# A larger load allowance in the instruction planner, and grouped output products in the gated linear attention

## The chip, the core and the metric

The kernel runs on one core of one Trainium2 chip. The time is device microseconds of one launch. A core has five instruction queues that the texts speak of: TensorE (PE; its weight loads are shown apart as PEld), VectorE (DVE), ScalarE (ACT), GpSimd (POOL) and SyncE (SP), which only issues DMA transfers. Each queue takes its instructions strictly in the order in which they were issued, and waits for semaphores of the others.

## The reference

One hybrid block in f32 on 512 latent tokens and 256 context tokens of width 1024, with two layers. Layer 0 has a bidirectional chunked gated linear attention (4 heads, 64 key and 128 value columns, chunks of 64 tokens) beside a gated spatial mixing; layer 1 has a bidirectional state-space scan. Every layer has modulated norms, gated residuals and a SwiGLU feed-forward. The part that the second edit touches is the output of the linear attention, for each direction:

```
b = cumsum(log_a, axis=2)
q_dec = q * exp(b)
o_inter = einsum('bnlhk,bnhkv->bnlhv', q_dec, s_prev)
scores = einsum('bnlhk,bnshk->bnhls', q_dec, k * exp(-b))
scores = where(tri, scores, 0.0)
o_intra = einsum('bnhls,bnshv->bnlhv', scores, v)
o = o_inter + o_intra
...
a = group_rms_norm(o, gla_norm_g, GLA_HEADS) * silu(r)
```

## The kernel before

The program is written once as a sequence of operations, and a planner orders them. `Plan._add` records each operation with its engine, its modelled cost and its dependencies; a block under `pl.together()` is recorded as one operation of TensorE, which nothing can be put into. `Plan.schedule` makes three rounds: `_forward` goes through modelled time and gives each engine, whenever it is free, the ready operation with the best key; `_backward` derives new keys from the order found. The order with the shortest modelled span is issued. On the chip nothing of the modelled times is left, only the order on each engine and the semaphores between engines. Since everything is issued from one line, all work shows as line 562 in the profile, and groups are told apart by tile names and shapes.

`LATENCY` is what the planner adds between the end of an operation and the readiness of a consumer on another engine. For "sync", a load, it stands behind the modelled transfer (`_cost`: bytes / 360e3 us, so 1.46 us for 512 KB and 0.73 for 256 KB).

Weights come through four 512 KB slots (`stg`): a load, then a split into two f16 halves, one by ScalarE and the rest by VectorE, into `gran` slots, from which TensorE multiplies in three passes. PSUM has eight banks, which the planner hands out. The adaLN rows are summed by VectorE from loads of `mod_w`.

The linear attention works on six tiles of 128 tokens with two chunks of 64 each. For each tile, scores of both directions are formed by small 64x64 products, and VectorE's masked copies bring them into `k2[i]` and empty the bank. Eleven steps then carry the state along the chunks, in both directions, by short VectorE operations of 64x128 on `S2`. In the output loop a tile's head gets one full product (scores times values, 128 columns of the array) and two half ones (decayed queries of one chunk times that chunk's state, 64 columns each), all into one bank:

```
for h in range(4):
    te.matmul(o[:, h, :], k2[i][:, h, :], vt[i][:, h * P:(h + 1) * P], start=True, stop=False)
    for c in range(2):
        te.matmul(o[64 * c:64 * c + 64, h, :], q2[i][:, h, 64 * c:64 * c + 64], S2[2 * i + c][:, h, :],
                  start=False, stop=True)
```

At the end of the kernel, each finished tile of 128 tokens has its squares summed by ScalarE, a reciprocal root made in short 128x1 steps by VectorE (`rstd_of`), and is multiplied by it and by `fgr`, the final norm's weights. The last tile is done in three pieces, whose products with `fgr` are separate operations.

Of the kernel before, what the change touches and what calls it, by code (L numbers as in the profile page):

```python
# [19 lines left out]
P = 128  # L20
# [200 lines left out]
PATIENCE = 0.14  # L221
MARGIN = 1.0
AHEAD = 4
LATENCY = {"tensor": 0.2, "vector": 0.25, "scalar": 0.35, "gpsimd": 0.3, "sync": 2.2}


class Plan:


    def __init__(self, nc):  # L230
        self.nc, self.ops, self.open, self.after, self.sooner, self.rush = nc, [], None, (), 0.0, 0.0
        for e in LATENCY:
            setattr(self, e, Engine(self, e))
# [22 lines left out]
    def _add(self, eng, calls):  # L256
# [19 lines left out]
        if eng == "sync":  # L276
            op.deps.update(self.after)
        op.lat = LATENCY[eng]
        self.ops.append(op)
# [102 lines left out]
    def _backward(self, order, span):  # L382
# [3 lines left out]
        for t, _, op in order:  # L386
            rank[op.idx] = -t - op.cost
        clock = dict.fromkeys(LATENCY, 0.0)
        ready = [0.0] * len(ops)
        wait = {e: [] for e in LATENCY}  # L390
        can = {e: [] for e in LATENCY}
        for op in ops:
            if not op.succ:
                heapq.heappush(wait[op.eng], (0.0, op.idx))
        for _ in ops:
            t, e = min((clock[e] if can[e] else max(clock[e], wait[e][0][0]), e) for e in LATENCY if can[e] or wait[e])
            while wait[e] and wait[e][0][0] <= t + 1e-9:
# [176 lines left out]
def tile_hybrid_block(ctx: ExitStack, tc: tile.TileContext, t_in: dict, out: bass.AP):  # L574
    nc = tc.nc
    pl = Plan(nc)
    va, sc, gp, te, sy = pl.vector, pl.scalar, pl.gpsimd, pl.tensor, pl.sync
# [37 lines left out]
    def at(off, shape, dt=F32):  # L615
        return area.view(off, shape, dt)
# [63 lines left out]
    o = ring_s((P, P))  # L680
# [4 lines left out]
    o = ring_s((P, 96))  # L685
# [97 lines left out]
    def rstd_of(ss, n, scale):  # L783
        t = smalls((P, 4, n))
        v, y, q, p = (t[:, i] for i in range(4))
        va.tensor_scalar(v, ss, 0.59565131 * scale, 0.59565131 * EPS, ALU.mult, ALU.add)
        va.tensor_scalar(y.bitcast(I32), v.bitcast(I32), -0.5, -553162335.0, ALU.mult, ALU.add)
        for last in (False, True):
            if n == 1:
                va.scalar_tensor_tensor(out=q, in0=y, scalar=y, in1=v, op0=ALU.mult, op1=ALU.mult)  # L790
            else:
                va.tensor_tensor(out=q, in0=y, in1=y, op=ALU.mult)
                va.tensor_tensor(out=q, in0=q, in1=v, op=ALU.mult)
            if last:
                va.scalar_tensor_tensor(out=y, in0=q, scalar=-1.59012754, in1=y, op0=ALU.add, op1=ALU.mult)
            else:
                va.scalar_tensor_tensor(out=p, in0=q, scalar=-1.98524553, in1=q, op0=ALU.add, op1=ALU.mult)
                va.scalar_tensor_tensor(out=y, in0=p, scalar=1.77101678, in1=y, op0=ALU.add, op1=ALU.mult)
        return y
# [116 lines left out]
    def split(src, dst):  # L916
        sc.activation(out=dst[0], in_=src, func=AF.Copy)
        va.tensor_tensor(out=dst[1], in0=src, in1=dst[0], op=ALU.subtract)

    def columns_of(src, dst):  # L920

        return src.rearrange("p (r c) -> p c r", r=8), [t.rearrange("p (c r) -> p c r", r=8) for t in dst]
# [56 lines left out]
    vt = [at(24 * KB + 2 * KB * i, (P, 512)) for i in range(NT)]  # L979
    q2 = [at(36 * KB + 2 * KB * i, (P, 4, P)) for i in range(NT)]  # L980
    k2 = [at(48 * KB + 2 * KB * i, (P, 4, P)) for i in range(NT)]
# [20 lines left out]
    for i in range(NT):  # L1002
        for k0 in (0, 4):
            o = ring_s((P, 4, P))
# [100 lines left out]
    o = ring_m((96, 256))  # L1105
    for kt in range(KT):
        with pl.together():
            for i, (a, b) in enumerate(PASSES):
                for g in range(3):
                    te.matmul(o[32 * g:32 * g + 32], wl[:, a, kt, :], hT(b, kt, slice(256 * g, 256 * g + 256)),  # L1110
                              start=(kt == 0 and i == 0), stop=(kt == KT - 1 and i == 2))
# [7 lines left out]
    for sl in (XS, CS):  # L1119
        n = sl.stop - sl.start  # L1120
        tl = slice(sl.start // P, sl.stop // P)
        for ws, which, scl in ((wk, 1, UN), (wq, 0, UN / 8.0)):
            for j in range(2):
                o = ring_m((P, n))
# [7 lines left out]
    for i in (4, 5, 0, 1, 2, 3):  # L1132
        o = ring_m((P, 512))
# [11 lines left out]
    for it, i in enumerate((4, 5, 0, 1, 2, 3)):  # L1145
# [32 lines left out]
        for c in range(2):  # L1178
            ch = 2 * i + c
            ds = ring_s((P, 4, P))  # L1180
            with pl.together():
                for h in range(4):
                    te.matmul(ds[:, h, :], kpt[64 * c:64 * c + 64, h, :], vt[i][64 * c:64 * c + 64, h * P:(h + 1) * P],
                              start=True, stop=True)
# [4 lines left out]
        for d in range(2):  # L1189
            o = ring_s((P, 4, 64))  # L1190
            with pl.together():
                for h in range(4):
                    for c in (0, 64):
                        te.matmul(o[c:c + 64, h, :], k2[i][64 * d:64 * d + 64, h, c:c + 64], q2[i][64 * d:64 * d + 64, h, c:c + 64],
                                  start=True, stop=True)
# [19 lines left out]
    o = ring_s((P, 4, P))  # L1215
# [7 lines left out]
    for i in range(NT):  # L1223
        o = ring_m((P, 512))
# [8 lines left out]
        o = ring_s((P, 4, P))  # L1233
# [6 lines left out]
    for j in range(4):  # L1240
        wu = w_cols(w_in, 1568 + j * P, P)
        for sl in (XS, CS):
            n = sl.stop - sl.start
            o = ring_m((P, n))
# [10 lines left out]
    for i in range(NT):  # L1255
        o = ring_m((P, 512))
# [5 lines left out]
    for i in range(NT):  # L1262
        o = ring_s((P, 4, P))
        with pl.together():
            for h in range(4):
                te.matmul(o[:, h, :], k2[i][:, h, :], vt[i][:, h * P:(h + 1) * P], start=True, stop=False)
                for c in range(2):
                    te.matmul(o[64 * c:64 * c + 64, h, :], q2[i][:, h, 64 * c:64 * c + 64], S2[2 * i + c][:, h, :],
                              start=False, stop=True)
        ss = smalls((P, 4))  # L1270
        junk, a = ts((P, 4, P)), ts((P, 4, P))
        for h in range(4):
            sc.activation(out=junk[:, h, :], in_=o[:, h, :], func=AF.Square, accum_out=ss[:, h:h + 1])
        r = rstd_of(ss, 4, 1.0 / P)
        for h in range(4):
            va.scalar_tensor_tensor(out=a[:, h, :], in0=o[:, h, :], scalar=r[:, h:h + 1], in1=rg[i][:, h * P:(h + 1) * P],
                                    op0=ALU.mult, op1=ALU.mult)
        if i < 4:
            latents.append(a)
        else:  # L1280
            o = ring_s((P, 4, P))
            with pl.together():
                for h in range(4):
                    te.transpose(o[:, h, :], a[:, h, :], ident)
            split(o, [t[:, :, TOK[i]] for t in aT_a])
        if i == 3:
            for h in range(4):
                o = ring_s((P, SEQ))
                with pl.together():
                    for t, a in enumerate(latents):  # L1290
                        te.transpose(o[:, TOK[t]], a[:, h, :], ident)
                split(*columns_of(o, [t[:, h, XS] for t in aT_a]))
# [30 lines left out]
    for i in range(NT):  # L1323
        for h in range(2):
            o = ring_m((P, 512))
# [121 lines left out]
    o = ring_s((P, 120))  # L1447
# [11 lines left out]
    for i in range(NT):  # L1459
        o = ring_m((P, 64))  # L1460
# [18 lines left out]
    def cum(mats):  # L1479
        o = ring_s((P, 2, NT, 32))  # L1480
        with pl.together():
            for d in range(2):
                te.matmul(o[:, d], mats[d], da[:, :, 32 * d:32 * d + 32], start=True, stop=True)
        return o
# [11 lines left out]
    o = cum(stri[::-1])  # L1496
# [3 lines left out]
    o = cum([ones, ones])  # L1500
    sc.activation(out=dec, in_=o, func=AF.Exp)
    o = ring_s((P, 4, P))
# [231 lines left out]
    for i in ffn(1, hS1, parts1, 4, (7, 7, 8), [(56 + 2 * k) * KB for k in range(8)], [4 * KB * k for k in (0, 1, 3, 4, 5, 8, 10, 11)], {0: gate5},  # L1734
                 pieces, ring_of([*range(40, 48, 2), *range(114, 120, 2)]), 1):
        o = t4[0]((P, D))
# [47 lines left out]
```

## Time and profile before

| | |
|---|---|
| time, median of 3 runs | 1624.97 us (1624.22 to 1628.23) |
| the profiled execution | 1628.33 us, of which the span is 1626.6 |
| TensorE busy | 1569.3 us (96%), granted clock 0.994 of full |
| VectorE busy | 1380.4 us (85%) |
| ScalarE busy | 945.9 us (58%) |
| moved by DMA | 210.53 MB, mean 129 GB/s |

The profiled execution is one run of the program; its span reaches from the first to the last instruction, and a little lies around it. A busy time counts an engine's instructions, not how well it is used by them.

### The profile page before, as it was taken

The numbers are of one execution on the slowest core, as the hardware profiler recorded it, in microseconds if no ns is written. First come the engines' busy times: TensorE is split into PE (matmuls) and PEld (weight loads), VectorE is DVE, ScalarE is ACT, GpSimd is POOL, SyncE is SP. The second block draws the span as 40 slices with busy tenths as digits, with TensorE's granted clock in tenths as the row PEclk, the third lists the DMA queues.
The fourth block names the chain that finished last, engine by engine and source line by source line (L and its number), as shares of the span: only waits on it lengthen the run. The fifth ranks groups of instructions, "written<-read, shape, count | busy, mean of one in ns | idle before, by whom it ended". The sixth has DMA issues, their size and how long they took to land. (4 is left out here: it accounts for less than half of the span.)

```text
span 1626.6 us, 28133 instructions
## 1 busy us (share of the span) xinstructions
PE 1569.3 (96%) x10893; PEld 949.0 (58%) x10893; DVE 1380.4 (85%) x2661; ACT 945.9 (58%) x1902; POOL 20.4 (1%) x65
## 2 busy tenths in 40 slices
PE   5999999999999999999999999999999999999997
PEld 3555655576545545555578555555544687786674
DVE  3899997699999989856569999999998898898775
ACT  6856534476424514523367899998875665464451
POOL 2000000000000000000010000000000000000000
PEclk9999999999999999999999999999999999999999
DMA  9663335015546565312312445454566233443321
GB/s 331 221 200 104 106 105 166 14 43 166 167 133 191 159 207 181 104 52 72 104 55 80 138 128 167 104 143 124 168 210 160 81 103 117 130 121 113 98 59 52
DMA packets 206121, 210.53 MB, mean 129 GB/s; under 512 B 27199, under 2 KB 154275, under 8 KB 205987
## 3 DMA queue, kind: packets, MB, share of 16 engines
q1 hardware_dynamic: 205987, 208.74, 43.0%
q8 instruction: 85, 1.39, 0.4%
q14 instruction: 49, 0.40, 0.1%
HBM read 197.01 MB, written 7.50 MB: 126 GB/s over the span
## 5 line engine op out<-in xcount | busy, mean ns | idle before, releaser
L562 PE MATMUL bank<-area,gran 128*128 128x256 f16 (+3 forms) x5604 | 788.8, 296 | 10.9 <-DVE area L562 6.3
L562 PEld LDWEIGHTS <-gran 128*128 128x128 f16 x5604 | 519.4, 98 | 260.6 <-issue 29.7
L562 PE MATMUL bank<-area 128*128 128x512 f16 (+9 forms) x3170 | 540.3, 327 | 9.6 <-ACT area L562 5.8
L562 PEld LDWEIGHTS <-area 128*128 128x128 f16 (+1 forms) x3270 | 303.3, 98 | 326.8 <-issue 30.2
L562 ACT ACTIVATE gran<-stg 128x512 f16<-128x512 f32 (+2 forms) x366 | 252.4, 699 | 227.7 <-PE bank L562 86.8
L562 ACT ACTIVATE area<-area 128x128 f32<-128x128 f32 (+8 forms) x557 | 249.0, 490 | 134.5 <-DVE area L562 121.0
L562 DVE TENSOR_TENSOR area<-area 128x512 f32<-128x512 f32 (+8 forms) x489 | 295.9, 627 | 28.1 <-ACT area L562 23.0
L562 ACT ACTIVATE area<-bank 128x384 f32<-128x384 f32 (+7 forms) x460 | 204.3, 463 | 180.7 <-PE bank L562 133.4
L562 DVE SCALAR_TENSOR_TENSOR gran<-stg,gran 128x512 f16<-128x512 f32 (+2 forms) x366 | 277.3, 774 | 32.5 <-ACT gran L562 30.4
L562 PE MATMUL bank<-gran,area 128*128 128x512 f16 (+1 forms) x1308 | 283.4, 360 | 4.4 <-DVE area L562 3.5
L562 DVE TENSOR_TENSOR area<-bank,area 128x512 f32<-128x512 f32 (+5 forms) x237 | 135.6, 581 | 70.8 <-PE bank L562 66.1
L562 DVE SCALAR_TENSOR_TENSOR area<-area,cs 128x512 f32<-128x512 f32 x224 | 158.0, 744 | 9.1 <-DMA area<-in_mod_w_dram 8.8
L562 DVE SCALAR_TENSOR_TENSOR area<-area,mrow 128x772 f32<-128x772 f32 (+1 forms) x96 | 91.6, 969 | 0.0
L562 PEld LDWEIGHTS bank<-area 128*64 128x64 f32 (+4 forms) x1208 | 72.9, 149 | 30.9 <-issue 10.3
L562 ACT ACTIVATE area<-stg 128x1024 f16<-128x1024 f32 (+1 forms) x56 | 55.4, 999 | 33.1 <-PE bank L562 15.6
L562 DVE SCALAR_TENSOR_TENSOR area<-stg,area 128x1024 f16<-128x1024 f32 (+1 forms) x56 | 64.2, 1152 | 11.0 <-ACT area L562 10.6
L562 ACT ACTIVATE area<-area,small 128x64 f32<-128x64 f32 (+1 forms) x161 | 62.0, 458 | 17.0 <-DVE small L562 16.1
L562 PE MATMUL bank<-ident,area 128*128 128x128 f32 (+1 forms) x351 | 51.5, 286 | 12.1 <-DMA area<-in_ssd_norm_g_dram 6.1
L562 DVE TENSOR_TENSOR stg<-stg,stg 128x512 f32<-128x512 f32 x88 | 60.2, 684 | 1.9 <-DMA stg<-in_ffn_w_in_dram 1.2
L562 DVE TENSOR_TENSOR stg<-stg 128x512 f32<-128x512 f32 x88 | 60.2, 684 | 0.5
L562 PEld LDWEIGHTS bank<-ident,area 128*128 128x128 f32 (+1 forms) x351 | 42.5, 147 | 23.7 <-issue 9.2
L562 DVE SCALAR_TENSOR_TENSOR area<-area 64x128 f32<-64x128 f32 (+3 forms) x148 | 52.5, 396 | 3.1 <-ACT area L562 2.5
(74 smaller groups left out, 567.3 us busy)
## 6 DMA issues: line engine op xcount, KB each, us to landing
area<-in_mod_w_dram SPq DMA_DIRECT2D x96, 512.0 KB, 4.3
stg<-in_ffn_w_in_dram SPq DMA_DIRECT2D x88, 512.0 KB, 4.7
stg<-in_ffn_w_out_dram SPq DMA_DIRECT2D x44, 512.0 KB, 3.7
stg<-in_ssd_w_in_dram SPq DMA_DIRECT2D x40, 512.0 KB, 3.9
area<-rowd SPq DMA_DIRECT2D x32, 512.0 KB, 3.9
stg<-in_ab_w_in_dram SPq DMA_DIRECT2D x20, 512.0 KB, 4.4
stg<-in_ssd_w_out_dram SPq DMA_DIRECT2D x32, 256.0 KB, 2.6
area<-in_x_dram SPq DMA_DIRECT2D x8, 512.0 KB, 5.1
```

Of the source, the lines that this page charges most:

```text
L562: getattr(eng, method)(*map(real, a), **{n: real(v) for n, v in k.items()})
```

## The change

The allowance that the planner adds behind a load goes from 2.2 to 4.0 us. In the output loop of the linear attention, a tile's four full products are issued first and the eight half ones after them; the first product of the bank starts its sum, and the others add to it.

```diff
-LATENCY = {"tensor": 0.2, "vector": 0.25, "scalar": 0.35, "gpsimd": 0.3, "sync": 2.2}
+LATENCY = {"tensor": 0.2, "vector": 0.25, "scalar": 0.35, "gpsimd": 0.3, "sync": 4.0}
...
         with pl.together():
             for h in range(4):
-                te.matmul(o[:, h, :], k2[i][:, h, :], vt[i][:, h * P:(h + 1) * P], start=True, stop=False)
+                te.matmul(o[:, h, :], k2[i][:, h, :], vt[i][:, h * P:(h + 1) * P], start=h == 0, stop=False,
+                          skip_group_check=True)
+            for h in range(4):
                 for c in range(2):
                     te.matmul(o[64 * c:64 * c + 64, h, :], q2[i][:, h, 64 * c:64 * c + 64], S2[2 * i + c][:, h, :],
-                              start=False, stop=True)
+                              start=False, stop=True, skip_group_check=True)
```

The planner's cost and dependencies of the tile's block are the same with both sequences, so its order is that of the first edit alone, but for the rows inside these blocks. The first edit moves instructions on all engines. Three places are shown.

The first place is TensorE's order at the first output tiles of the linear attention (`bank_N` is a PSUM bank, and `area` the scratch memory in which scores, queries, values and states lie). Before, one tile and the start of the next:

```order
L562 MATMUL bank_67<-area 128x128 [waits DVE_49,Pool_49]
L562 MATMUL bank_67<-area 64x128 x2
L562 MATMUL bank_67<-area 128x128
L562 MATMUL bank_67<-area 64x128 x2
L562 MATMUL bank_67<-area 128x128
L562 MATMUL bank_67<-area 64x128 x2
L562 MATMUL bank_67<-area 128x128
L562 MATMUL bank_67<-area 64x128 x2
L562 MATMUL bank_70<-area 128x128 [waits DVE_49,Pool_49]
```

After, two tiles and what follows:

```order
L562 MATMUL bank_69<-area 128x128 [waits DVE_49,Pool_49]
L562 MATMUL bank_69<-area 128x128 x3
L562 MATMUL bank_69<-area 64x128 x8
L562 MATMUL bank_65<-area 128x128 [waits Activation_49,Pool_49]
L562 MATMUL bank_65<-area 128x128 x3
L562 MATMUL bank_65<-area 64x128 x8
L562 LDWEIGHTS area
```

A tile goes through eight changes between full and half products before, and two after.

The second place is VectorE's order at the last scores of the linear attention: masked copies that empty score banks, and steps of the chunk scan (64x128) and additions of both directions (64x4x64) between them. Before:

```order
L562 COPY_PREDICATED area<-area,bank_70 64x4x64
L562 TENSOR_TENSOR area<-area 64x4x64 [waits DVE_49]
L562 SCALAR_TENSOR_TENSOR area<-area 64x128 [waits Activation_49]
L562 SCALAR_TENSOR_TENSOR area<-area 64x128 x3
L562 TENSOR_TENSOR area<-area 64x4x64 [waits DVE_49] x2
L562 SCALAR_TENSOR_TENSOR area<-area 64x128 [waits DVE_49] x12
L562 TENSOR_TENSOR area<-area 64x4x64
L562 SCALAR_TENSOR_TENSOR area<-area 64x128 [waits Activation_49]
L562 SCALAR_TENSOR_TENSOR area<-area 64x128 x3
L562 COPY_PREDICATED area<-area,bank_64 64x4x64 [waits Pool_49]
L562 COPY_PREDICATED area<-area,bank_66 64x4x64 [waits PE_49]
```

After:

```order
L562 COPY_PREDICATED area<-area,bank_68 64x4x64
L562 TENSOR_TENSOR area<-area 64x4x64 [waits DVE_49] x2
L562 SCALAR_TENSOR_TENSOR area<-area 64x128 [waits Activation_49]
L562 SCALAR_TENSOR_TENSOR area<-area 64x128 x3
L562 TENSOR_TENSOR area<-area 64x4x64 [waits DVE_49] x2
L562 SCALAR_TENSOR_TENSOR area<-area 64x128 [waits Activation_49]
L562 SCALAR_TENSOR_TENSOR area<-area 64x128 x3
L562 SCALAR_TENSOR_TENSOR area<-area 64x128 [waits DVE_49] x4
L562 COPY_PREDICATED area<-area,bank_68 64x4x64 [waits PE_49]
L562 COPY_PREDICATED area<-area,bank_68 64x4x64
```

Before, 20 scan steps and four additions stand ahead of the next bank that is emptied; after, 12 and four, and then `bank_68` is emptied alone. TensorE's next score group into `bank_68` stands behind three earlier groups and six products with 256 columns.

The third place is VectorE's order at the end of the kernel: the residual additions of the last tile (reading a bank), the scaling of the tile before it (128x1024), the products with the final norm's weights (last tile, from `area` alone) and the sum over the last tile's pieces (TENSOR_REDUCE). Before:

```order
L562 TENSOR_REDUCE small_87<-small_87 128x1 [waits Activation_49]
L562 SCALAR_TENSOR_TENSOR small_86<-small_86 128x1 [waits DVE_49]
L562 TENSOR_SCALAR small_88<-small_87 128x1 [waits DVE_49]
L562 SCALAR_TENSOR_TENSOR small_86<-small_86 128x1 [waits DVE_49]
L562 TENSOR_SCALAR small_88<-small_88 128x1 [waits DVE_49]
L562 SCALAR_TENSOR_TENSOR area<-area,small_86 128x1024 [waits DMAHW4_49,DVE_49]
L562 SCALAR_TENSOR_TENSOR small_88<-small_88 128x1 [waits DVE_49]
L562 TENSOR_TENSOR area<-area 128x256 [waits DMAHW5_49]
L562 SCALAR_TENSOR_TENSOR small_88<-small_88 128x1 [waits DVE_49]
L562 TENSOR_TENSOR area<-area 128x512
L562 SCALAR_TENSOR_TENSOR small_88<-small_88 128x1 [waits DVE_49]
L562 TENSOR_TENSOR area<-area 128x256
```

After:

```order
L562 SCALAR_TENSOR_TENSOR area<-area,small_86 128x1024 [waits DMAHW4_49,DVE_49]
L562 TENSOR_TENSOR area<-bank_69,area 128x512 [waits PE_49]
L562 TENSOR_TENSOR area<-area 128x512 [waits DVE_49]
L562 TENSOR_TENSOR area<-bank_63,area 128x256 [waits PE_49]
L562 TENSOR_TENSOR area<-bank_70,area 128x256 [waits PE_49]
L562 TENSOR_TENSOR area<-area 128x256 [waits DVE_49] x2
L562 TENSOR_TENSOR area<-area 128x256 [waits DMAHW5_49,DVE_49]
L562 TENSOR_TENSOR area<-area 128x256 [waits DVE_49]
L562 TENSOR_TENSOR area<-area 128x512
L562 TENSOR_REDUCE small_87<-small_87 128x1 [waits Activation_49]
L562 TENSOR_SCALAR small_88<-small_87 128x1 [waits DVE_49]
```

The scaling of the tile before the last stood behind the sum, and now stands ahead of the last residual additions; the three products with the norm's weights stood behind the sum, and now stand ahead of it.

## Rows read from the trace of the kernel before

**Rows 1.** The page's first part: busy us, share of the span, instructions.

```profile
PE 1569.3 (96%) x10893; PEld 949.0 (58%) x10893; DVE 1380.4 (85%) x2661; ACT 945.9 (58%) x1902; POOL 20.4 (1%) x65
```

**Rows 2.** Windows: length, busy us of PE, PEld, DVE, ACT, POOL; clock, DMA share, GB/s.

```profile
0.00:40.00 40.00, 22.06 (x298) 15.49 (x298) 14.67 (x48) 24.65 (x43) 9.47 (x39) 0.91 0.97 332
200.00:240.00 40.00, 36.55 (x327) 21.90 (x326) 38.64 (x96) 13.82 (x33) 2.10 (x4) 0.96 0.26 80
240.00:280.00 40.00, 40.00 (x229) 21.37 (x229) 31.19 (x101) 19.15 (x54) 0.00 (x0) 1.00 0.63 182
280.00:320.00 40.00, 40.00 (x197) 19.24 (x196) 22.90 (x50) 14.78 (x23) 0.00 (x0) 1.00 0.04 16
320.00:1600.00 1280.00, 1259.74 (x8672) 775.20 (x8671) 1101.51 (x1966) 763.92 (x1570) 6.53 (x18) 1.00 0.42 124
880.00:1240.00 360.00, 350.12 (x2224) 191.92 (x2222) 341.75 (x589) 315.50 (x717) 0.00 (x0) 1.00 0.51 147
```

**Rows 3.** Timeline of PE at output tiles: start, us, instruction, count, idle before.

```profile
231.24 9.42 PE L562 MATMUL bank<-area 128*128 128x128 f32 x72
240.59 5.35 PE L562 MATMUL bank<-gran,area 128*128 128x512 f16 x24
245.78 3.12 PE L562 MATMUL bank<-area 128*128 128x128 f32 x24
248.83 8.59 PE L562 MATMUL bank<-gran,area 128*128 128x512 f16 x39
```

**Rows 4.** Timeline of PE at spatial mixing (full) and cumulative sums (half).

```profile
159.34 1.05 PE L562 MATMUL bank<-area 128*128 128x128 f32 x8
160.23 1.03 PE L562 MATMUL bank<-gran,area 128*128 128x512 f16 x4
...
76.13 1.09 PE L562 MATMUL bank<-area 128*64 128x128 f32 x16
77.15 0.82 PE L562 MATMUL bank<-area,gran 128*128 128x512 f16 x3
```

**Rows 5.** Timeline of PE at the last scores.

```profile
207.77 1.62 PE L562 MATMUL bank<-area 64*64 64x64 f32 x48
...
218.18 4.13 PE L562 MATMUL bank<-gran,area 128*128 128x512 f16 x12 [3.19 <-DVE area L562]
222.15 0.82 PE L562 MATMUL bank<-area,gran 128*128 128x256 f16 x6
```

**Rows 6.** Timeline of DVE at the last scores.

```profile
201.94 1.77 DVE L562 TENSOR_TENSOR area<-area 64x256 f32<-64x256 f32 x4
...
205.87 3.73 DVE L562 COPY_PREDICATED area<-area,bank 64x256 f32<-64x256 uint8 x8
...
212.06 3.31 DVE L562 SCALAR_TENSOR_TENSOR area<-area 64x128 f32<-64x128 f32 x12
```

**Rows 7.** Waits: who waited for what, us in total, times, longest.

```profile
ACT gran L562 <- DMA stg<-in_ffn_w_in_dram: 79.2, 47, 6.5
...
PE bank L562 <- DVE area L562: 15.7, 20, 3.2
```

**Rows 8.** Timeline of DVE at the kernel's end.

```profile
1617.82 0.15 DVE L562 TENSOR_REDUCE small<-small 128x1 f32<-128x3 f32 x1
...
1618.38 1.28 DVE L562 SCALAR_TENSOR_TENSOR area<-area,small 128x1024 f32<-128x1024 f32 x1
...
1619.72 0.42 DVE L562 TENSOR_TENSOR area<-area 128x256 f32<-128x256 f32 x1
...
1620.12 0.68 DVE L562 TENSOR_TENSOR area<-area 128x512 f32<-128x512 f32 x1
...
1621.57 0.48 DVE L562 TENSOR_SCALAR area<-area,small 128x512 f32<-128x512 f32 x1
```

**Rows 9.** DMA issues of the page: count, KB each, median us to landing.

```profile
stg<-in_ffn_w_in_dram SPq DMA_DIRECT2D x88, 512.0 KB, 4.7
...
stg<-in_ssd_w_out_dram SPq DMA_DIRECT2D x32, 256.0 KB, 2.6
```

## The prediction

> **What bounds the kernel now.** I begin with the totals per engine on the page [rows 1]: TensorE is busy 1569.3 of 1626.6 us and VectorE 1380.4. So TensorE is the engine whose work sets the length, and a stretch in which it is not busy, or busy with avoidable work, is where time can be had. The windows [rows 2] say where that is: 17.9 us of the first 40 are without TensorE work (loads are awaited there), 3.45 us of 200 to 240, and 20.3 us of the long middle from 320 to 1600, 9.9 of these from 880 to 1240. From 240 to 320 TensorE has no gap, while VectorE has 8.8 and 17.1 us to spare. That matters, since the second edit stands there. The table of waits [rows 7] gives what TensorE waited for: 15.7 us for VectorE in 20 waits. ScalarE waits far longer for loads, 79.2 us in 47 times, but little of that reaches TensorE. The two edits therefore have to be looked at in two ways: the products cut TensorE's own work in a stretch where it sets the pace; the planner's number moves everything else, and its worth lies in the waits.
>
> **The products of the linear attention's output.** In the timeline [rows 3] one token tile is a run of 24 records: an f32 matmul leaves two, so four full products are 8 and eight half ones are 16. Three tiles follow each other from 231.24 to 240.59, 3.12 us each; a fourth takes 245.78 to 248.83, 3.05 us. I take 3.08 for each of the six. What would the same work cost in blocks of one form? Rows of other stages show both forms [rows 4]. Eight records with full columns stand at 159.34 and the next product starts at 160.23: 0.89 us. Sixteen with 64 columns stand at 76.13 and the next starts at 77.15: 1.02 us, which are two to an interval of some 0.11, because the halves write to different columns of the array and run side by side. Together 1.91 us. The 1.17 us that a tile now takes above this go with its eight changes of form (each head goes from full to half and back), 0.146 us each. After the change there are two, into the halves and out of them. If the cumsum row already holds both, a tile costs 1.91; if neither, 2.20. I take 2.0, nearer the row, which stands between f16 products with full columns and so has both changes in it. The gain is 6 x (3.08 - 2.00) = **6.5 us**, with ends 6 x 0.88 = 5.3 and 6 x 1.17 = 7.0. In the order of the change the first two such tiles still stand in a row, and each is one block of 4 and one of 8 rows. Does it reach the end? TensorE has no gap from 240 to 320, so its shorter work moves up what follows, as long as VectorE follows; its 25.9 spare us there [rows 2] hold 6.5, and also the 12 accumulations of the modulation rows that the new order moves to behind this stage.
>
> **The planner's number.** It changes no instruction's work. What it does is to count a 512 KB load's consumer as ready 1.8 us later, so that other work is put ahead of it in the engines' fixed orders, on all engines. Nothing in the kernel then waits for 4 us: an engine takes its next instruction when its semaphores allow it. So only places can be costed where the order shows a different wait.
>
> *Score stage.* Now TensorE waits 3.19 us at 218.18 [rows 5], for a bank that VectorE's masked copies empty, and these stand behind a dozen short scan steps of the linear attention (3.31 us) and some more [rows 6]. The twelve products behind the wait take 3.97 us to the next row, where at the pitch of the same form (24 from 240.59 to 245.78, 0.216 us each [rows 3]) they would take 2.59: for part of them the granted clock is the lower level, 1.2 GHz, after the idle time. That price of 1.4 us any such stall may pay, and I leave it in both kernels. In the order of the change the last score group of a tile (`bank_68`) waits for copies that stand behind four additions of 64x256 (1.77 us) and twelve scan steps (3.31); with two copies at 3.73 / 8 = 0.47 that makes 6.0 us. TensorE, which waits for the copies ahead of these steps, has meanwhile two score groups (three in 1.62 us at 207.77 [rows 5]) and six products of 256 columns (half of 0.216 each), together 1.7 us. The stall would be about 4.3 us instead of 3.2: **+1**, with ends of 0 (if VectorE arrives there earlier in its order than TensorE) and +2.5 (if the lower clock comes on top for longer).
>
> *Tail.* After the last products VectorE now does work of finished tiles inside the chain that ends the kernel [rows 8]. From the sum at 1617.82 to the last scaling at 1621.57 lie short dependent steps, between them a scaling of a whole tile (1.28 us) and three multiplications (0.42 twice and 0.68), 2.8 us of work that isn't the chain's. In the order of the change the tile's scaling stands ahead of the last residual additions, where VectorE waits for TensorE anyway, and the three multiplications stand ahead of the sum. The first goes, about 1.2 us; the others overlap the ScalarE squares that the sum waits for, but hold the sum up by some 0.6. I take **-1.5**, ends 0 and -2.
>
> *Start.* The fourth tile of x is loaded ahead of the modulation weights, and the second eight of these start five places later behind 768 KB of other loads, 2.3 us at the 332 GB/s of the first window [rows 2]; against that, the bias and the first half's scale come earlier, and later loads have less ahead of them. I take **0**, ends -1.5 and +2.4.
>
> *Elsewhere.* The feed-forward and the state-space stages are reordered throughout, with the same work. TensorE's gaps from 320 to 1600 are 20.3 us [rows 2]. I can't say from the order which of them open or close; I take **0** with ends -10 and +10, half of them closed or half as many again. Against the direction of the edit one row speaks: a feed-forward load lands a median 4.7 us after its issue and a 256 KB one of the state-space output 2.6 [rows 9]; the plan counted 3.66 and 2.93 for these, and now 5.46 and 4.73. The truth lies between for the one and below both for the other: by the rows the new number overshoots the feed-forward's landing by 0.8 where the old one undershot it by 1.0. The Trainium skill's page "DMA: Bandwidth & Descriptors", section "Anatomy of one DMA — SWDGE (gpsimd) path", fits a load's time as 2.0 us plus bytes over 436 GB/s; 512 KB would be an estimated 3.2 us, so that the old number fits and the new one counts over 2 us too many for every load. The trace disagrees for the feed-forward's loads (4.7) and agrees for the smaller ones (an estimated 2.6 by the page, 2.6 measured).
>
> **Sum.** -6.5 + 1 - 1.5 + 0 + 0 = -7.0 us, against the profiled execution's 1628.33 (span 1626.6): 1621.3. That execution lies 3.4 above the median of the runs shown, 1624.97, so the forecast for the median is **1618.0**. The likeliest case alone has 1613 to 1623.
>
> **Rivals.**
> - *The plan now holds loaded work back* (slower). Place: 880 to 1240, where TensorE (350.1 of 360), VectorE (341.8) and ScalarE (315.5) are all nearly full [rows 2]. With 256 KB loads there in 2.6 us and counted as 4.73, splits of weights are put behind the scan's work although their load is long in, and TensorE's products wait for the split. If its 9.9 us without work double and some more, +14, the kernel takes 1632. For it: a load of the order of 2 us too early costs nothing, a split too late costs its wait on the full engine. Against it: TensorE's 15.7 us of waits for VectorE [rows 7] have no load as their last cause. It decides from +11.8 on, where 1629.8 is passed.
> - *The replanning also closes gaps.* Feed-forward loads at 4.7 are late by the old count, ScalarE waits 79.2 us for them, and products queue behind the splits. With 8 to 10 of the middle's 20.3 us closed: 1608 to 1610.
> - *The product's gain does not get through.* VectorE has only 1.4 us to spare from 200 to 240 and 18 of the 360 from 880 on [rows 2]. If it, not TensorE, sets the pace there, the 6.5 us shrink to about 1 and the result is 1623.5, within 0.3%. Against it: TensorE is at 40.00 in two windows in between, with VectorE at 31.19 and 22.90.
> - *The regrouping does nothing.* If a half product takes its 0.2 us whatever stands ahead of it, 1624.5. Against it: the cumsum's halves [rows 4] run at half of that.
>
> **How the numbers follow.** A difference under 0.3% (4.9 us: 1620.1 to 1629.8) is no change here. Chances: the forecast 0.44, of which a fifth ends over 1620.1; gaps closed as well 0.18; gain swallowed 0.18; regrouping idle 0.05; held back 0.15, all but a little of it past 1629.8. Faster: 0.35 + 0.18 + 0.02 of the swallowed = 0.55; within: 0.09 + 0.16 + 0.05 + 0.02 of the held back = 0.32; slower 0.13. The range of 8 in 10 reaches from the closed gaps' upper part, 1609, to 1629, which leaves the held-back case and the best of the closed gaps out.
>
> **What would show it.** Products: each of the six runs of 24 records takes 2.0 us (1.91 to 2.20). Scores: TensorE's longest wait near 215 for VectorE goes from 3.2 to about 4.3. Tail: no scaling of a tile between the last sum and the last scaling, and 1.5 us less from the last product to the end. Elsewhere: TensorE's idle time from 320 to 1600 stays within a few us of 20, and ScalarE's waits for feed-forward loads fall without TensorE's waits moving. The prediction is wrong if TensorE's gaps from 880 to 1240 grow or shrink by more than 8 us, or if VectorE has no slack left behind the products.

## The result

The changed kernel takes 1601.9 us (median of 4 runs, 1599.86 to 1602.25) against 1626.6 of before: ratio 0.9844, interval 0.9823 to 0.9866. It is 24.7 us faster. The forecast of 1618.0 had the direction, not the size, and its range ended 7 us above the result. The profiled execution has a span of 1600.5 us, 26.1 less than before's. The first line of its page, with the columns of [rows 1]:

```profile
PE 1557.1 (97%) x10893; PEld 949.7 (59%) x10893; DVE 1380.8 (86%) x2661; ACT 939.6 (59%) x1900; POOL 20.7 (1%) x65
```

VectorE has the work that it had [rows 1]. TensorE is busy for 12.2 us less, and the span shrank by more than that. The windows of the changed kernel, with the columns of [rows 2], show where it also stands still less:

```profile
0.00:80.00 80.00, 61.29 (x605) 38.17 (x606) 52.00 (x112) 56.50 (x99) 10.62 (x41) 0.96 0.86 280
200.00:240.00 40.00, 35.35 (x247) 20.24 (x248) 37.33 (x94) 15.57 (x27) 1.05 (x2) 0.91 0.27 89
320.00:1580.00 1260.00, 1251.23 (x8648) 772.49 (x8647) 1104.01 (x1979) 758.93 (x1570) 6.96 (x18) 1.00 0.43 125
880.00:1220.00 340.00, 337.68 (x2166) 183.64 (x2164) 331.13 (x585) 308.14 (x708) 0.00 (x0) 1.00 0.55 156
```

From 320 us to just before the tail, TensorE is idle for 8.8 us where it was 20.3 [rows 2], and in the state-space part of it for 2.3 instead of 9.9. The fall from 320 us on is the largest piece, and the forecast had put 0 there. The products' tiles, the rows of which answer to [rows 3]:

```profile
230.27 2.08 PE L562 MATMUL bank<-area 128*128 128x128 f32 x24
232.28 1.04 PE L562 MATMUL bank<-gran,area 128*128 128x512 f16 x4
...
251.72 2.08 PE L562 MATMUL bank<-area 128*128 128x128 f32 x24
253.73 3.41 PE L562 MATMUL bank<-gran,area 128*128 128x512 f16 x15
```

A tile takes 2.01 us, read from its first row to the next row, as before's 3.08 were; the two tiles that stand in a row take 4.12 together. The tail, in VectorE's rows that answer to [rows 8]:

```profile
1591.20 0.76 DVE L562 TENSOR_TENSOR area<-bank,area 128x256 f32<-128x256 f32 x2 [0.87 <-PE bank L562]
1591.87 2.02 DVE L562 TENSOR_TENSOR area<-area 128x256 f32<-128x256 f32 x5
1593.81 0.15 DVE L562 TENSOR_REDUCE small<-small 128x1 f32<-128x3 f32 x1
...
1595.46 0.48 DVE L562 TENSOR_SCALAR area<-area,small 128x512 f32<-128x512 f32 x1
```

From the sum to the last scaling pass 1.65 us instead of 3.75, and no tile is scaled in between.

### The profile page after: what moved, and what is told of

It is laid out like the page before. It is cut to its first block, busy times and chain, and to the rows that moved or that the text cites. A ratio compares the mean times of both kernels' runs of the same rounds, so it can differ in the third digit from the quotient of the medians.

```text
span 1600.5 us, 28106 instructions
## 1 busy us (share of the span) xinstructions
PE 1557.1 (97%) x10893; PEld 949.7 (59%) x10893; DVE 1380.8 (86%) x2661; ACT 939.6 (59%) x1900; POOL 20.7 (1%) x65
## 4 chain that ended last, share of the span: by engine, by line
PE 78%; DVE 12%; ACT 6%; DMA 2%; issue 1%; SPq 0%; DVEq 0%; ACTq 0%
PE bank L562 78%; DVE area L562 9%; ACT area L562 5%; DVE gran L562 2%; ACT gran L562 1%; ACT L560 1%; DMA area<-in_mod_b_dram 1%; DMA area<-in_mod_w_dram 1%; ACT L562 1%; DVE small L562 0%; DVE stg L562 0%; DMA area<-area 0%; DMA stg<-in_ffn_w_in_dram 0%; DMA area<-in_x_dram 0%; DMA stg<-in_ssd_w_out_dram 0%
## 5 line engine op out<-in xcount | busy, mean ns | idle before, releaser
L562 PE MATMUL bank<-area,gran 128*128 128x256 f16 (+3 forms) x5604 | 780.7, 296 | 3.0 <-DVE area L562 2.6
L562 PE MATMUL bank<-area 128*128 128x512 f16 (+9 forms) x3170 | 525.8, 326 | 8.4 <-DVE area L562 5.5
L562 PEld LDWEIGHTS <-area 128*128 128x128 f16 x3270 | 303.5, 98 | 324.1 <-issue 19.1
L562 ACT ACTIVATE area<-bank 128x384 f32<-128x384 f32 (+8 forms) x460 | 204.8, 465 | 189.4 <-PE bank L562 140.6
L562 DVE SCALAR_TENSOR_TENSOR area<-area 64x128 f32<-64x128 f32 (+3 forms) x148 | 53.8, 395 | 3.7 <-ACT area L562 2.6
```

The source lines that it names most:

```text
L562: getattr(eng, method)(*map(real, a), **{n: real(v) for n, v in k.items()})
```

## Where the old order lost time: two chains

Before the experiments I looked for a gap of TensorE that the changed kernel no longer has. At 426.61 us of the kernel before, one row of each of three engines shows how a load reaches TensorE without being named as the cause of its wait (the timelines of ScalarE, VectorE and TensorE; in brackets the idle time and who ended it):

```profile
424.74 0.63 ACT L562 ACTIVATE gran<-stg 128x512 f16<-128x512 f32 x1 [2.62 <-DMA stg<-in_ffn_w_in_dram]
...
425.40 0.69 DVE L562 SCALAR_TENSOR_TENSOR gran<-stg,gran 128x512 f16<-128x512 f32 x1 [1.86 <-ACT gran L562]
426.01 0.55 DVE L562 TENSOR_TENSOR area<-bank,area 128x384 f32<-128x384 f32 x1
...
426.61 1.62 PE L562 MATMUL bank<-area,gran 128*128 128x384 f16 x9 [1.50 <-DVE area L562]
```

The plan put the split of a weight tile where its load should have landed. It had not. ScalarE waited 2.62 us at the split, VectorE 1.86 for ScalarE's half, and behind VectorE's half stood an addition that reads a bank. TensorE waited 1.50 us, by the profile for VectorE. A second chain of this kind starts at a load of modulation weights, for which VectorE waits:

```profile
604.46 1.54 DVE L562 SCALAR_TENSOR_TENSOR area<-area,cs 128x512 f32<-128x512 f32 x2 [2.61 <-DMA area<-in_mod_w_dram]
...
609.90 0.75 DVE L562 SCALAR_TENSOR_TENSOR area<-area,cs 128x512 f32<-128x512 f32 x1 [0.66 <-DMA area<-in_mod_w_dram]
...
611.84 0.43 PE L562 MATMUL bank<-area,one 128*32 128x128 f32 x8 [0.87 <-DVE area L562]
```

From these came the theory: with 2.2 the loads were counted as landed too early, the orders put splits and accumulations ahead of work that was ready, and TensorE paid at second or third hand. Its rival: the planner reorders nearly every row at any change of a number, the old order was a poor draw, and any other number would have done as well.

## The experiments

All times are medians; "before" was run beside each on the same chip and took 1625.4 to 1627.4, so kernels that were not run beside each other compare to some 2 us. But for allowance_alone, all kernels have the regrouped products.

**The two edits apart.** The first kernel has the new sequence of products alone; against the changed kernel its edit is

```diff
-LATENCY = {"tensor": 0.2, "vector": 0.25, "scalar": 0.35, "gpsimd": 0.3, "sync": 4.0}
+LATENCY = {"tensor": 0.2, "vector": 0.25, "scalar": 0.35, "gpsimd": 0.3, "sync": 2.2}
```

> Regrouped output products with the allowance left at 2.2. By the prediction's term the six tiles go from 3.08 to 2.0 us and the kernel is 5.3 to 7.0 us faster than before, about 1620 beside 1626.6. Rival, that the products' gain does not get through: within 1 us of before. If it gives more than 10 us, the replanning is not what made the change larger than forecast.

Measured: 1617.2 us, ratio 0.9948 (0.9932 to 0.9963), 8.5 us faster by the ratio, with 6.0 to 11.1 in the interval. Its tiles take what they take in the changed kernel, so the forecast's 6.5 lies in the interval; from 840 to 1240 us TensorE still idles for 9.9:

```profile
241.13 2.08 PE L562 MATMUL bank<-area 128*128 128x128 f32 x24
243.14 8.59 PE L562 MATMUL bank<-gran,area 128*128 128x512 f16 x39
...
840.00:1240.00 400.00, 390.14 (x2665) 224.26 (x2662) 378.53 (x652) 343.79 (x764) 0.00 (x0) 1.00 0.50 143
```

The second kernel has the new allowance alone; against the kernel before its edit is

```diff
-LATENCY = {"tensor": 0.2, "vector": 0.25, "scalar": 0.35, "gpsimd": 0.3, "sync": 2.2}
+LATENCY = {"tensor": 0.2, "vector": 0.25, "scalar": 0.35, "gpsimd": 0.3, "sync": 4.0}
```

> The allowance of 4.0 with the old sequence of products. If replanning closed gaps of TensorE between 320 and 1240 us, as the changed kernel's windows suggest (20.3 us of the middle without work against 8.8), this is 17 to 20 us faster than before, about 1608. If the two edits only help together, under 10 us.

Measured: 1607.55 us, ratio 0.9885 (0.9869 to 0.9901): 18.7 us. So the allowance carries about two thirds or more, and the two edits add up to the whole within their intervals.

**The size of the allowance.** One number of the changed kernel differs (2.0, 2.3, 3.0, 3.9, 5.0 in place of 4.0).

> Both edits, allowance 2.0, further below the measured landing. Theory of the loads' count: 1616 to 1622, slower than or equal to the 1617 of 2.2, with TensorE's gaps from 320 to 840 at 4 us or more. Theory of draws: as likely below 1612 as above.

> Both edits, allowance 2.3, a tenth above the old number. Theory of loads placed too early: the loads are counted almost as early as with 2.2, so the time stays within 4 us of the 1617 that the products alone gave, with ScalarE's waits for feed-forward loads at 60 us or more. Rival, that any new number draws a new order and 2.2 was a poor draw: 5 us or more away from 1617, most likely below it.

> Both edits, allowance 3.0 instead of 4.0: the plan counts 4.46 us for a 512 KB load, near the median of 4.0 to 4.7 measured. Theory of loads placed too early by the old count: nearly all of the gain, 1600 to 1608. Rival, that any new number only shuffles the order: anywhere between 1600 and 1630, with no relation to ScalarE's waits for loads.

> Both edits, allowance 3.9, a tenth below the new number. Theory of loads placed too early: within 4 us of the 1601.9 of the changed kernel. Rival, that 4.0 was a good draw: 5 us or more slower, about 1607 to 1615.

> Both edits, allowance 5.0: the plan counts 6.46 us for a 512 KB load, more than the median landing. Theory of loads placed too early: as fast as with 4.0 within 5 us, since an early load costs nothing while slots are free, and ScalarE's waits for feed-forward loads stay under 30 us. Rival, that too large a number holds loaded work back: slower than with 4.0 by 8 us or more, with TensorE's gaps from 880 to 1220 above 6 us.

Measured, with the time in which TensorE had no work in three stretches (the window's length less its busy time) and ScalarE's wait for feed-forward input weights:

| allowance | time, us | 320 to 840 | 840 to 1240 | 1320 to 1590 | ScalarE's wait |
|---|---|---|---|---|---|
| 2.0 | 1636.0 | 13.6 | 6.4 | 3.7 | 96.6 |
| 2.2 (products alone) | 1617.2 | 4.4 | 9.9 | 0.7 | 69.9 |
| 2.3 | 1615.8 | 4.4 | 5.4 | 0.6 | 77.0 |
| 3.0 | 1607.7 | 0.8 | 1.6 | 0.0 | 53.8 |
| 3.9 | 1603.2 | 1.8 | 2.9 | 0.5 | 33.0 |
| 4.0 (the change) | 1601.9 | 0.6 | 2.3 | 0.8 | 25.4 |
| 5.0 | 1625.1 | 3.5 | 3.4 | 14.0 | 19.0 |

The time falls from 2.0 to 4.0 without an exception. A tenth beside the old number gives the old time within 1.4 us, a tenth beside the new one the new time within 1.3 (1 and 3 by the ratios to before). Between 2.2 and 4.0 this is what the theory of the count expects, and not what draws would give. The idle time of a single stretch doesn't follow the number so evenly: from 840 to 1240 it is 9.9 us at 2.2, 5.4 at 2.3 and 6.4 at 2.0.

At 2.0 the expectation, 1616 to 1622, missed by 14 us. The direction is the theory's, but two tenths less cost 19 us where one tenth more gained 1.4, and why the loss there is so steep is not shown. The kernel is slower than before in spite of its faster products; its waits for loads, with the waiting tile first, are

```profile
ACT gran L562 <- DMA stg<-in_ffn_w_in_dram: 96.6, 47, 7.4
...
DVE area L562 <- DMA area<-in_mod_w_dram: 15.8, 14, 5.9
```

where the changed kernel has

```profile
ACT gran L562 <- DMA stg<-in_ffn_w_in_dram: 25.4, 12, 5.9
...
DVE area L562 <- DMA area<-in_mod_w_dram: 2.0, 3, 0.8
```

At 5.0 the loss comes from the other side. Its expectation (within 5 us of 4.0) missed: 23 us slower. ScalarE waits least for loads there, and TensorE stands still for 14.0 us in the last feed-forward stage. By the table of waits 8.2 of these are for ScalarE's or VectorE's half of a split, while neither engine waits there for a load of feed-forward input weights: the splits come late, not the loads (timeline of TensorE):

```profile
1345.02 0.39 PE L562 MATMUL bank<-area,gran 128*128 128x256 f16 x2 [1.24 <-ACT gran L562]
1346.16 10.79 PE L562 MATMUL bank<-area,gran 128*128 128x256 f16 x82 [0.75 <-DVE gran L562]
...
1361.76 0.39 PE L562 MATMUL bank<-area,gran 128*128 128x256 f16 x2 [1.24 <-ACT gran L562]
1362.90 9.13 PE L562 MATMUL bank<-area,gran 128*128 128x256 f16 x82 [0.75 <-DVE gran L562]
```

**Draws.** To see how far a number without meaning moves the time, ScalarE's own allowance was changed by a hundredth, at 2.2 and at 4.0:

```diff
-LATENCY = {"tensor": 0.2, "vector": 0.25, "scalar": 0.35, "gpsimd": 0.3, "sync": 4.0}
+LATENCY = {"tensor": 0.2, "vector": 0.25, "scalar": 0.36, "gpsimd": 0.3, "sync": 4.0}
```

> Both edits, allowance 2.2, and ScalarE's own allowance 0.36 instead of 0.35: a change of no meaning that draws another order. Theory that the old order's state-space stage was a poor draw: TensorE's time without work from 840 to 1240 falls from the 9.9 us of the products alone to 6 or less, and the time is 1607 to 1613. Theory that the count of the loads makes it: within 3 us of 1617.

> Both edits, allowance 4.0, and ScalarE's own allowance 0.36 instead of 0.35. If 4.0 was a good draw: 1606 or more. If the loads' count makes the gain: within 4 us of 1601.9, with 320 to 840 us nearly without gaps of TensorE.

Measured: 1615.6 us at 2.2 (1617.2 without) and 1604.6 at 4.0 (1601.9 without). The draws are real ones: matched by operation, tile name and shape, 58% of VectorE's rows keep their sequence in either, where the change itself leaves 45%. Yet the time moves by 1.6 and 2.7 us (3.4 and 2.3 by the ratios to before). With before's 2.2 the stretch from 840 to 1240 keeps 8.2 us without work. So the rival, the poor draw, falls as the main cause between 2.2 and 4.0. In these two pairs and the two neighbours above, a draw is worth some 3 us; that none is worth more is not shown.

**Which loads.** The allowance was set by what a transfer reads, here 4.0 for the feed-forward weights and 2.2 for the rest:

```diff
-LATENCY = {"tensor": 0.2, "vector": 0.25, "scalar": 0.35, "gpsimd": 0.3, "sync": 4.0}
+LATENCY = {"tensor": 0.2, "vector": 0.25, "scalar": 0.35, "gpsimd": 0.3, "sync": 2.2}
...
         op.lat = LATENCY[eng]
+        if eng == "sync" and "ffn" in getattr(getattr(calls[0][2]["in_"], "tensor", None), "name", ""):
+            op.lat = 4.0
```

> Both edits, 4.0 for the 132 feed-forward loads alone and 2.2 for all others. If the gain sits in loads of the first feed-forward stage: the gaps of TensorE from 320 to 840 (7 us more in the old order) close, and 1608 to 1612 comes out. If the state-space stage's loads carry it: about 1615 to 1618, as with the products alone.

> Both edits, 2.2 for the 132 feed-forward loads and 4.0 for all others. If the state-space stage's loads carry the larger part (its gaps fell from 9.9 to 2.3 us): 1605 to 1610, with ScalarE's waits for feed-forward loads back above 60 us. If the feed-forward loads carry it: about 1613 or more.

> Both edits, 4.0 only for the 96 loads of the modulation weights, which are spread from the start to the state-space stage, 2.2 for all else. If they carry the gain, through the start and VectorE's order: 1605 to 1610. By the theory of round trips: about 1615.

> Both edits, 4.0 only for the 73 loads of the state-space stage's input and output weights, 2.2 for all else. If late weights (the chain of the old order ends two waits on loads of the output weights between 1185 and 1224) carry the gain: 1605 to 1610. If the round trips do: about 1615.

> Both edits, 4.0 only for the 128 transfers whose source is the kernel's own data (transposes by DMA, and the ways through DRAM of the scan's rows, the scan's outputs and the residual), 2.2 for all loads of inputs. Theory: these come in chains in the state-space stage, so their short allowance is paid several times; if they carry the gain, 1605 or less. If the loads of weights carry it: within 4 us of the 1617 of the products alone.

> Both edits, 4.0 for all loads of inputs and 2.2 for the 128 transfers of the kernel's own data, which alone at 4.0 made it 4 us slower. If the kinds add up: 1598 to 1602, as fast as the changed kernel or faster. If they don't: 1603 to 1612.

Measured, 4.0 for the kind named and 2.2 for the rest: feed-forward weights 1613.4, modulation weights 1608.7, state-space weights 1614.6, the kernel's own data 1621.2; all but the feed-forward weights 1602.1; all inputs 1605.2. Against 1617.2 that is 3.8, 8.5 and 2.6 us gained and 4.0 lost for single kinds. The theory that round trips are paid several times missed: alone they cost. The feed-forward weights and the state-space weights missed the gains that were expected if they carried it. Two pairs of these kernels split all loads between them: feed-forward weights and all others gained 3.8 and 15.1, inputs and own data 12.0 and -4.0. The change has 15.3, so the kinds don't simply add. With draws of 3 us on every one of these numbers, of the single kinds only the modulation weights' gain stands well clear.

One thing speaks against too simple a reading. With all loads but the feed-forward's at 4.0, ScalarE waits 86.7 us for feed-forward weights, TensorE stands still for 4.5 us from 320 to 840 as with the old number, and the kernel is as fast as the changed one:

```profile
ACT gran L564 <- DMA stg<-in_ffn_w_in_dram: 86.7, 40, 5.9
```

So the sum of an engine's waits for loads is no price, and the chain at 426.61, which starts at a feed-forward load, shows how a load can reach TensorE, not where the gain lies: with that kind left at 2.2 none of the gain is lost. What should count is whether something that TensorE needs stands behind the waiting instruction; this is argued, no run tests it.

**The upper end.** 5.0 for all loads but the feed-forward's, which have 4.0:

```diff
         op.lat = LATENCY[eng]
+        if eng == "sync" and "ffn" in getattr(getattr(calls[0][2]["in_"], "tensor", None), "name", ""):
+            op.lat = 4.0
...
-LATENCY = {"tensor": 0.2, "vector": 0.25, "scalar": 0.35, "gpsimd": 0.3, "sync": 4.0}
+LATENCY = {"tensor": 0.2, "vector": 0.25, "scalar": 0.35, "gpsimd": 0.3, "sync": 5.0}
```

> Both edits, 4.0 for the 132 feed-forward loads and 5.0 for all others. With 5.0 for all, TensorE stood still for 18 us in the last feed-forward stage. If it is the feed-forward loads' own number that holds their splits back, this stage has under 3 us of waits again and the time is 1602 to 1607; if it is the order that the other loads' number draws, the 18 us stay and the time is above 1617.

Measured: 1605.7 us. Of the 14.0 us of the last feed-forward stage (the trace doesn't give the 18 of the expectation) 1.4 are left, as the window shows. As far as one kernel can show it, it was the feed-forward loads' own number that held their splits back:

```profile
1320.00:1590.00 270.00, 268.61 (x1985) 193.83 (x1984) 218.41 (x405) 136.32 (x273) 0.00 (x0) 1.00 0.34 100
```

None of these kernels is clearly faster than the changed one.

## Why the prediction was wrong

- **Products, forecast -6.5:** right. Tiles went from 3.08 to 2.01 us, 6 x 1.07 = 6.4 us, and the kernel with this edit alone gained 8.5, with 6.0 at the interval's lower end. The reading behind it, that the price lies in the changes of form, fits: six fewer per tile gave 1.07 us, 0.18 each, where I had divided out 0.146. The edit also has only the first product of a bank start its sum, and no run parts the two. The Trainium skill's page "TensorEngine Tiling (Array Packing)", section "Key Properties", says that changing the tiling mode drains the engine. The trace agrees in so far as fewer changes took less time; a drain as such it doesn't show. The rivals that the gain does not get through, or isn't there, fall with this kernel.
- **Score stage, forecast +1:** the size fits and the place doesn't, so the fit is luck. Idle time from 200 to 240 us grew from 3.45 to 4.65. But the last score group (16 products of 64x64) ran at 212.56 with no wait; the wait is ten us earlier, ahead of products of 64 rows, 2.87 us for VectorE (the line at 202.79 in the last section). I had counted VectorE's rows from a point at which it would stand ready, and VectorE itself waited 1.66 us for TensorE there:

```profile
212.56 0.68 PE L562 MATMUL bank<-area 64*64 64x64 f32 x16
...
211.61 1.83 DVE L562 COPY_PREDICATED area<-area,bank 64x256 f32<-64x256 uint8 x4 [1.66 <-PE bank L562]
```

- **Tail, forecast -1.5:** right in mechanism, and near in size. From the last residual additions out of the banks (before's row below) to the end it was 1626.6 - 1615.6 = 11.0 us, and is 1600.5 - 1591.2 = 9.3, 1.7 less. From TensorE's last product to the end, which the prediction had named as the sign, it was 11.5 and is 9.0: 2.5 less, half a microsecond beyond the end that I had set.

```profile
1615.59 0.75 DVE L562 TENSOR_TENSOR area<-bank,area 128x256 f32<-128x256 f32 x2
```

- **Start, forecast 0:** somewhat off. In the first 80 us TensorE is busy 61.29 us where it was 58.76, 2.5 us won, beyond the end of -1.5 that I had set. From 80 to 200 us, for which the forecast had no term, 1.4 us of idle time came back. Before's window:

```profile
0.00:80.00 80.00, 58.76 (x595) 35.81 (x596) 49.99 (x109) 59.22 (x107) 10.73 (x41) 0.94 0.84 276
```

- **Elsewhere, forecast 0 with ends of 10:** this step failed. The idle time from 320 on fell by 11.5 us, which is the changed kernel's rival "the replanning also closes gaps", priced at 8 to 10 and given a chance of 0.18. The 0 stood on "I can't say from the order", and on the sentence that little of ScalarE's 79.2 us of waits for loads reaches TensorE. I took it from the table of waits, where from 320 us on TensorE's own waits name VectorE and ScalarE but for 0.8 us. Those are the last releasers only: the chains at 426.61 and 611.84 show a load one or two steps behind such a wait. That this step failed is shown by the allowance alone, which gained 18.7 us with the old products. (By the sign that the prediction had set, a move of more than 8 us from 880 to 1240, it would just have passed: 9.9 became 2.3.)

The row on landings had been a hint: 4.7 us measured against 3.66 counted. But a median of that view rests on the few transfers whose landing the trace gives, here 12 of 88. These took 3.79 to 7.85 us; all are longer than the old count of 3.66, and nine are shorter than the new one of 5.46. Of the modulation weights 9 of 96 are known, 3.92 to 9.59 us, again none within the old count:

```profile
area<-in_mod_w_dram SPq DMA_DIRECT2D x96, 512.0 KB, 4.3
```

A count at the median would still be too early for half of the loads, which may be why 4.0 (5.46 us, above both medians) beat 3.0 (4.46, between them); this is argued, not shown. The overshoot that I worked out from 4.7 did no visible harm at 4.0. (The fit that the prediction quotes for a load's time is, by the title of its section, one for transfers issued from GpSimd; these loads are SyncE's, so the rows neither confirm nor refute it.)

- **The rival "held back"** did not come at 4.0, but it exists. At 5.0 it costs 14 us of TensorE's time in the last feed-forward stage, not in the state-space stage where I had placed it.

Of the span's 26.1 us, 13.9 are idle time of TensorE: -2.5 up to 80 us, +1.4 to 200, +1.2 to 240, -11.5 from 320 to the tail, and -2.5 in the tail. The other 12.2 are its busy time. The tiles are 6.4 of these; the remaining 5.8 spread over many groups of products, as pauses too short to be told from work, and I can't assign them. The lower clock is not their source: outside the tail, TensorE is busy at a granted clock of 0.50 for 10.3 us before and 10.9 after. What is shown is that between 2.2 and 4.0 the time follows the number that the loads are counted with, and not the draw; that every single one of the closed gaps was a load's doing is argued from two chains, not shown.

## What to carry to other kernels

A planner's allowance for loads should be held against measured landings, the late ones too and not the median alone, and be swept: here 2.0 to 4.0 was worth 34 us and 5.0 gave back 23. Before calling waits for loads harmless, follow a few waits of the bound engine back two steps; the table of waits names only the last releaser. And, as here, products on differently shaped parts of the array should be issued in blocks of one shape when they go into one bank anyway.

## What the runs showed of the hardware

Loads of the same 512 KB land at quite different times: those of the feed-forward's input weights whose landing is known took 3.79 to 7.85 us before (12 of 88, median 4.7 [rows 9]) and 3.82 to 5.83 in the changed kernel (6 of 88). With so few known, the lower median there doesn't show that landings became faster:

```profile
stg<-in_ffn_w_in_dram SPq DMA_DIRECT2D x88, 512.0 KB, 4.0
```

A change between full and half columns of the array costs f32 products about 0.18 us each, if the tile's whole gain of 1.07 us is put down to its six changes. After the wait of 2.87 us, eight records that take 1.16 us elsewhere took 2.08, at a granted clock of 0.50, the level of 1.2 GHz; so this stall cost more than itself:

```profile
195.11 1.16 PE L562 MATMUL bank<-area 64*128 64x128 f32 x8
...
202.79 2.08 PE L562 MATMUL bank<-area 64*128 64x128 f32 x8 [2.87 <-DVE area L562]
...
202.80:204.80 2.00, 2.00 (x9) 1.78 (x9) 1.91 (x6) 0.00 (x0) 0.00 (x0) 0.50 0.00 0
```

Not every such stall does. Before, the wait of 3.19 us at 218.18 [rows 5] was followed by twelve products in 3.97 us, with the granted clock at 0.50 up to 221.01. In the kernel with the products alone a wait of the same length at the same place was followed by the same twelve in 2.59 us, with the granted clock at 1.00 throughout:

```profile
218.02 2.75 PE L562 MATMUL bank<-gran,area 128*128 128x512 f16 x12 [3.19 <-DVE area L562]
220.61 0.82 PE L562 MATMUL bank<-area,gran 128*128 128x256 f16 x6
```
